# The output projection of an attention layer's last two quarters as seven block products

## The chip, the cores and the metric

The kernel runs on one core of a Trainium2 chip. The metric is device time in microseconds (us) of one execution of the whole program. The kernel before takes 2368.16 us, the median of three runs between 2368.03 and 2368.29.

## The reference

One layer of a streaming encoder on 2048 tokens of width 1024, in float32: an attention in chunks of 64 tokens (each reads its own chunk and the eight before it, 16 heads of 64) with an output projection, then a dense SwiGLU network of inner width 2816. Both are wrapped in two RMS norms.

```python
h = rms_norm(x, g_pre_mix)
o = attention(h, w_qkv, rel_bias)             # softmax(q k / 8 + bias) v, 16 heads merged to 1024
x = x + rms_norm(o @ w_o, g_post_mix)
h = rms_norm(x, g_pre_ffn)
x = x + rms_norm((silu(h @ w_gate) * (h @ w_up)) @ w_down, g_post_ffn)
```

The change is about `o @ w_o`, 1024 by 1024, and what reads its result.

## The kernel before, in words

Everything is kept transposed: a tile has 128 features in its partitions and 512 tokens in its columns. The 2048 tokens are four quarters of 512 (`NQ`) and two groups of 1024 (`NG`). A float32 product is three matmuls of 512 columns (`products`, L195): each operand is split in a high part (ScalarE) and a low part (VectorE), and high by high, high by low and low by high are added in one bank of PSUM. Below, such three matmuls are a triple.

Most large products use a scheme of Strassen and Winograd: operands are cut in two by two blocks, and seven block products with sums of blocks (named B11, B21, T1, T2, B22, T3, T4 for the column side, A11, A12, S1 to S4, A22 for the weight side) stand in for eight. The projections of q, k and v do so, the gate and up products (`gate_up`, L995) and the down product. The output projection does not: `o_quarter` (L632) runs, for one quarter, eight output tiles with eight triples each, 64 triples, and ends every tile with a copy to DRAM (`o_d`) and a square added to the row sum (`osums`) that the later norm needs.

The stages follow each other: q, k, v for both groups; the attention of the quarters in the order 1, 0, 2, 3 (`SEQ_OF`); a dense stage; the FFN of group 0 (gate and up in eleven chunks of 56 triples, then down) and of group 1. A quarter of the attention has eight jobs, one per pair of heads, of four slots each, one per block of 128 queries (loop at L1635). A slot issues the transposes of one block (`transposed`, L571), in every second slot the transposes of the fifth key block, the scores of the block three slots ahead (`scores`, L522) and a share of the dense work at hand (`fill`, L1613). After the fourth slot of a pair comes its output product (`output`, L605), whose result ScalarE copies as high part and VectorE as low part into `ats`. From the second quarter on, both heads of a pair write their scores to one tile of three PSUM banks (`later_banks`, L459). The dense work between a quarter's scores is the output projection of the quarter before; the first quarter has none, and the projection of the last quarter is the dense stage behind the attention. There VectorE and ScalarE also build the first columns B11, B21 and T1 of the FFN (`Blocks.build`, L721), with their parts of x1 loaded as L11 to L22.

What sets the order: TensorE's is the order of the program text. Steps of other engines are queued in `later` with a cost each and issued as the generators of TensorE's work advance (`tick`, L206, one unit per triple); a scheduler places them on their engines, with the steps of the softmax and the output copies put ahead. Loads and most stores go through one queue, SyncE's (SP), in order; stores of weight sums and additions in DRAM go through GpSimd's (POOL). Weight tiles come from `take` (L177) with splits at fixed triples (`part_split`, L151) in the attention, and from a `Stream` (L889) that loads six items ahead and splits three ahead elsewhere. `weight_sums` (L862) forms the S blocks of the down weights by copies and adding transfers within DRAM, one step per eight triples, 40 of them in the projection stage, the rest in the first FFN. `Late` (L1188) adds a quarter's projection to x: from `osums` (`rows`) or from sums formed anew out of `o_d` (`sums`, `rstd`), and `write`.

## Time and profile before

| | |
|---|---|
| median of three runs | 2368.16 us |
| profiled execution: its time / its span | 2367.66 us / 2365.9 us |
| busy over the span: PE, PEld | 2318.8 us (98%), 1898.9 us (80%) |
| DVE, ACT, POOL | 1634.0 us (69%), 1141.5 us (48%), 324.5 us (14%) |
| mean granted TensorE clock | 0.996 |
| DMA | 531.80 MB, mean 225 GB/s |

PE is TensorE's matmuls, PEld its weight loads, DVE is VectorE, ACT ScalarE, POOL GpSimd, SP SyncE. Times within the execution count from its first instruction. Matmuls are pipelined: the duration of a record is longer than the step from one start to the next, and the steps are what a sum is made from. The bracket at the end of a row gives the idle time of the engine before it and what ended it. Names such as `tt`, `pd` or `hb` are tiles; `po`, the output product's bank, appears as `tt`.

The last quarter's attention lies from 882 to 1041.5 us, the dense stage from there to 1086.2, the first chunk of gate and up to 1124.3.

### The profile page before, as it was taken

The page shows a single profiled execution, that of the slowest core. Times are in us where ns is not written, and L with a number is a line of the kernel's source. Part 1 is how long each engine was busy: PE and PEld are TensorE (multiplying, and loading weights), DVE is VectorE, ACT ScalarE, POOL GpSimd, SP SyncE. Part 2 cuts the span into 40 slices and gives each one's busy share as a digit, 9 for nine tenths or more (in the row PEclk, how much of TensorE's full clock was granted, in tenths as well). Part 3 has the DMA queues.
Part 4 walks back from the last instruction along what each step waited for, and adds up shares of the span by engine and source line. Part 5 has one row for each costly group of instructions (what it writes and reads, how often), then busy time and mean ns, then how long its engine had stood idle before and what let it go on. Part 6 is the DMA issues. An engine that isn't in the chain of part 4 may idle for free.

```text
span 2365.9 us, 32865 instructions
## 1 busy us (share of the span) xinstructions
PE 2318.8 (98%) x11456; PEld 1898.9 (80%) x11456; DVE 1634.0 (69%) x2620; ACT 1141.5 (48%) x1979; POOL 324.5 (14%) x426
## 2 busy tenths in 40 slices
PE   9999999989999999999999999999999999999998
PEld 7788888877777778778888888888888888888886
DVE  8787856667566665769786877667657676555577
ACT  7544643367666566665323333455433333334444
POOL 1000011044333433511100000000000000000001
PEclk9999999999999999999999999999999999999999
DMA  8777799998897888766876454567666656547654
GB/s 302 250 254 270 241 280 263 281 261 232 218 254 218 242 261 253 240 216 221 281 245 215 168 200 152 178 209 249 222 226 194 216 171 225 155 164 233 196 189 145
DMA packets 231509, 531.80 MB, mean 225 GB/s; under 512 B 26512, under 2 KB 42912, under 8 KB 226864
## 3 DMA queue, kind: packets, MB, share of 16 engines
q1 hardware_dynamic: 219440, 482.52, 64.1%
q0 software_dynamic: 11904, 47.19, 7.0%
q8 instruction: 90, 1.47, 0.3%
q14 instruction: 75, 0.61, 0.1%
HBM read 382.23 MB, written 170.44 MB: 234 GB/s over the span
## 4 chain that ended last, share of the span: by engine, by line
PE 68%; DVE 2%; DMA 2%; ACT 1%; issue 1%; POOL 0%; SPq 0%; DVEq 0%
PE pd L197 6%; PE pd L199 6%; PE pd L198 6%; PE pb L197 5%; PE pb L199 5%; PE pb L198 5%; PE tt L618 3%; PE pc L197 3%; PE pc L198 3%; PE pa L198 3%; PE pc L199 3%; PE pa L199 3%; PE pa L197 3%; PE tt L582 2%; PE mm L197 2%; PE mm L199 2%
## 5 line engine op out<-in xcount | busy, mean ns | idle before, releaser
L567 POOL TENSOR_SCALAR sc<-sc,rows 128x640 f32<-128x640 f32 (+4 forms) x256 | 199.1, 792 | 303.9 <-DVE rows L563 240.2
L553 ACT ACTIVATE sc<-sc,rows 128x640 f32<-128x640 f32 (+4 forms) x256 | 193.2, 757 | 91.6 <-DVE rows L548 90.5
L197 PE MATMUL pb<-hb,w_wg_T 128*128 128x512 f32 x528 | 205.9, 390 | 1.2 <-DVE terms L1045 1.1
L199 PE MATMUL pb<-hb,w_wg_T 128*128 128x512 f32 x528 | 205.4, 389 | 0.0
L198 PE MATMUL pb<-hb,w_wg_T 128*128 128x512 f32 x528 | 205.4, 389 | 0.0
L548 DVE CUSTOM_DVE_ANT_0 sc<-st,bias 128x640 f32<-128x640 f32 (+2 forms) x248 | 174.1, 734 | 45.2 <-PE st L539 19.6
L538 PE MATMUL st<-k,q 128*128 128x384 f32 (+3 forms) x432 | 138.4, 337 | 13.3 <-DVE rows L548 11.4
L586 DVE COPY pT<-tt 128x512 f32<-128x512 f32 (+3 forms) x128 | 81.7, 638 | 84.5 <-PE tt L582 82.8
L199 PE MATMUL pd<-a,w_d_T 128*128 128x512 f32 (+1 forms) x368 | 139.8, 380 | 0.1
L197 PE MATMUL pd<-a,w_d_T 128*128 128x512 f32 (+1 forms) x368 | 139.9, 380 | 0.0
L198 PE MATMUL pd<-a,w_d_T 128*128 128x512 f32 (+1 forms) x368 | 139.7, 380 | 0.0
L197 PE MATMUL pa<-hb,w_wg_B 128*128 128x512 f32 x352 | 136.9, 389 | 0.0
L198 PE MATMUL pa<-hb,w_wg_B 128*128 128x512 f32 x352 | 136.9, 389 | 0.0
L199 PE MATMUL pa<-hb,w_wg_B 128*128 128x512 f32 x352 | 136.9, 389 | 0.0
L582 PEld LDWEIGHTS tt<-ident,sc 128*128 128x128 f32 x928 | 105.2, 140 | 37.2 <-POOL sc L567 15.7
L131 ACT ACTIVATE w_wg_T<-raw 128x1024 fp32r<-128x1024 f32 x88 | 93.1, 1058 | 80.0 <-PE pa L199 34.5
L582 PE MATMUL tt<-ident,sc 128*128 128x128 f32 x928 | 125.8, 275 | 5.3 <-DVE rows L563 2.5
L539 PE MATMUL st<-k,q 128*128 128x384 f32 (+3 forms) x432 | 125.6, 311 | 0.0
L289 POOL TENSOR_TENSOR rs<-ms,neg_half 128x4 f32<-128x4 f32 (+1 forms) x7 | 7.5, 1072 | 856.8 <-DVE ms L287 856.8
L357 DVE TENSOR_TENSOR a<-raw_a,a 128x512 fp32r<-128x512 f32 x154 | 105.8, 694 | 26.8 <-ACT a L356 26.7
L1047 ACT ACTIVATE terms<-terms 128x512 f32<-128x512 f32 x65 | 41.1, 632 | 170.5 <-DVE terms L1045 170.4
L618 PE MATMUL tt<-pT,v 128*64 128x512 f32 (+3 forms) x832 | 119.9, 438 | 0.0
(277 smaller groups left out, 6171.5 us busy)
## 6 DMA issues: line engine op xcount, KB each, us to landing
raw<-in_w_gu SPq DMA_DIRECT2D x77, 512.0 KB, 4.2
q<-q SPq DMA_DIRECT2D x62, 512.0 KB, 6.4
k<-k SPq DMA_DIRECT2D x54, 512.0 KB, 8.1
s_g_S<-raw POOLq DMA_DIRECT2D x44, 512.0 KB, 3.0
raw_d<-d_S SPq DMA_DIRECT2D x88, 256.0 KB, 3.7
raw_a<-aT SPq DMA_DIRECT2D x88, 256.0 KB, 3.8
raw<-s_g_S SPq DMA_DIRECT2D x44, 512.0 KB, 4.0
bias<-ext_d SPq DMA_DIRECT2D x124, 144.0 KB, 8.9
```

The source lines that it names most:

```text
L131: act.activation(hi, raw, AF.Copy)
L197: pe.matmul(pt, a_hi, b_hi, start=first, stop=False, skip_group_check=go_on)
L198: pe.matmul(pt, a_hi, b_lo, start=False, stop=False, skip_group_check=go_on)
L199: pe.matmul(pt, a_lo, b_hi, start=False, stop=last, skip_group_check=go_on)
L357: eng.tensor_tensor(lo, src, hi.bitcast(F32), op=ALU.subtract)
L538: pe.matmul(st[:, a:b], q[:, 2 * h, cols], kk[:, h, key], start=True, stop=False)
L539: pe.matmul(st[:, a:b], q[:, 2 * h + 1, cols], kk[:, h, key], start=False, stop=True)
L548: dve.tensor_tensor_reduce(out=sc[:, :n], in0=st[:, c0 : c0 + n], in1=rev, scale=-1.0, scalar=3.0e38, op0=ALU.add, op1=ALU.min, accum_out= ...
L553: act.activation(sc[:, :n], sc[:, :n], AF.Exp, bias=nmax, scale=-1.0, accum_out=rows[:, h : h + 1])
L567: last_pool[0] = pool.tensor_scalar(sc[:, :n], sc[:, :n], rows[:, 2 + h : 3 + h], 1.0, op0=ALU.mult, op1=ALU.mult)
L582: pe.transpose(tt[:, u, :], sc[h][:, b * P : b * P + P], ident)
L618: pe.matmul(po[heads[h], c0:c1], v[:, kb, c : c + 64], self.pT[:, h, r, c0:c1], start=m == 0, stop=m == len(terms) - 1,)
```

## The change

The last two quarters (2 and 3 in order of tokens, the third and fourth to be worked on) are taken as two column blocks of one product, the halves of the features as the other cut, and the scheme of seven block products replaces the two runs of 64 triples. A block product is four output tiles with four triples each.

- Two products, A11 and A12 by the third quarter's own columns, run between the scores of the last quarter (`o_first`); the first is kept in DRAM as p1, the second added to it gives the upper output rows of the third quarter.
- Five, S1, S2, S3, S4 and A22 by T1, T2, T3, B22 and T4, run in the dense stage (`o_rest`); here these column names mean differences of the two quarters' attention outputs. T1 is prepared in the slots of the last quarter, T2, T4, T3 and B22 during the first of the five. Results are formed on VectorE from p1 and the banks.
- The third quarter's output is stored a second time, in float32, to `at_d`, and loaded again for the differences (`Columns`); the fourth is kept in float32 without a low part.
- The S blocks of the output weights are formed by `weight_sums` ahead of the down weights', in two pieces of 128 by 1024.
- The FFN's first columns B11, B21 and T1 are issued later in the dense stage, into other tiles.
- Row sums of the last two quarters no longer come from the projection; `Late` forms them from `o_d` in the first FFN.

```diff
...
+    at_d = dram.tile([P, KT, HALF], F32, name="at")
+    p1_d = dram.tile([P, 4, HALF], F32, name="p1")
+    sum_o = {n: [dram.tile([P, 1024], F32, name=f"o_{n}_{c}") for c in range(2)] for n in ("S1", "S2", "S3", "S4")}
...
-    plan = [w_o[c] for c in range(4)] * NQ
+    halves_of = [w_o[c][:, n : n + 1024] for c in range(4) for n in (0, 1024)]
+    o_at = {n: [halves_of[i], halves_of[i + 2]] for n, i in (("A11", 0), ("A12", 1), ("A21", 4), ("A22", 5))}
+    plan = [halves_of[2 * c : 2 * c + 2] for c in range(4)] * (NQ - 2) + [o_at["A11"], o_at["A12"], sum_o["S1"]]
...
-            sp.dma_start(part, plan[n][:, here])
+            sp.dma_start(part, plan[n][c])
...
+            if n == SEQ_OF[-1]:
+                if p == 0:
+                    ats[n] = hb_tile(2, F32, (KT, HALF))
+                with tc.high_priority(offset=400):
+                    act.activation(ats[n][:, p, :], po, AF.Copy)
+                return lambda: None
             if p == 0:
                 ats[n] = Cols(((0, 1), (2, 3))[SEQ_OF.index(n) % 2])
             with tc.high_priority(offset=400):
                 act.activation(ats[n].hi(p), po, AF.Copy)
+            if n == SEQ_OF[-2]:
+                t = io("at")
+                with tc.high_priority(offset=400):
+                    act.activation(t, po, AF.Copy)
+                sp.dma_start(at_d[:, p, :], t)
...
     def o_quarter(n):
 
         src = ats[n]
-        last = n == SEQ_OF[-1]
         osums[n] = row_tile("osum", f"osum_{n}") if SEQ_OF.index(n) % 2 else const.tile([P, HALF], F32, name=f"osum_{n}", tag="osum", bufs=1)
...
-            if last and d2 == KT // 2 - 1:
-                back.ahead(-2)
...
+    def o_first(src):
+
+        for half in range(2):
+            w = take()
+            for d in range(4):
+                pt = dense_bank(d)
+                if half:
+                    p1 = io("p1")
+                    sp.dma_start(p1, p1_d[:, d, :])
+                for k in range(4):
+                    hi, lo = w.tiles[d // 2]
+                    c = slice(k * 256 + d % 2 * P, k * 256 + d % 2 * P + P)
+                    products(pt, hi[:, c], lo[:, c], src.hi(4 * half + k), src.lo(4 * half + k), k == 0, k == 3)
+                    yield 3 * C512
+                    if (d, k) == (2, 3):
+                        part_split(0)
+                    elif (d, k) == (3, 2):
+                        part_split(1)
+                if half:
+                    dve.tensor_tensor(p1, p1, pt, op=ALU.add)
+                    sp.dma_start(o_d[SEQ_OF[-2]][:, d, :], p1)
+                else:
+                    t = io("y")
+                    act.activation(t, pt, AF.Copy)
+                    sp.dma_start(p1_d[:, d, :], t)
+
+    class Columns:
+
+
+        def __init__(self):
+            self.at2 = hb_tile(3, F32, (KT, HALF))
+            self.at3 = None
+            self.t = {}
+
+        def load(self, half):
+            here = slice(4 * half, 4 * half + 4)
+            sp.dma_start(self.at2[:, here, :], at_d[:, here, :])
+
+        def t1(self, k):
+            dve.tensor_tensor(self.at2[:, k, :], ats[SEQ_OF[-1]][:, k, :], self.at2[:, k, :], op=ALU.subtract)
+
+        def others(self, k, which=range(3)):
+            at2, at3 = self.at2, ats[SEQ_OF[-1]]
+            if 0 in which:
+                dve.tensor_tensor(at2[:, k, :], at3[:, 4 + k, :], at2[:, k, :], op=ALU.subtract)
+            if 1 in which:
+                dve.tensor_tensor(at2[:, 4 + k, :], at2[:, 4 + k, :], at2[:, k, :], op=ALU.subtract)
+            if 2 in which:
+                dve.tensor_tensor(at3[:, k, :], at3[:, k, :], at3[:, 4 + k, :], op=ALU.subtract)
+
+        def put(self, name, k):
+            slot, src, at, sign = {
+                "T1": (0, self.at2, k, 1), "T2": (1, self.at2, k, 1), "T4": (6, self.at2, 4 + k, 1),
+                "T3": (4, ats[SEQ_OF[-1]], k, 1), "B22": (5, ats[SEQ_OF[-1]], 4 + k, -1),
+            }[name]
+            if name not in self.t:
+                self.t[name] = hb_tile(slot)
+            hi, lo = (self.t[name][:, n, k, :] for n in range(2))
+            if sign > 0:
+                split(hi, lo, src[:, at, :])
+                return
+            act.activation(hi, src[:, at, :], AF.Copy, scale=-1.0)
+            dve.scalar_tensor_tensor(lo, src[:, at, :], -1.0, hi.bitcast(F32), op0=ALU.mult, op1=ALU.subtract)
+
+    def o_items():
+
+        def load(src):
+            t = phase["fp"].tile([P, 1024], F32, tag="w4", name="raw4", bufs=phase["w4"])
+            sp.dma_start(t, src)
+            return t
+
+        def make(name, t):
+            w = w_tile(f"o_{name}")
+            split_part(*w, t)
+            return w
+
+        return [
+            (lambda src=src: load(src), lambda t, n=n, c=c: make(f"{n}_{c}", t), 6, 3)
+            for n, both in (("S2", sum_o["S2"]), ("S3", sum_o["S3"]), ("S4", sum_o["S4"]), ("A22", o_at["A22"]))
+            for c, src in enumerate(both)
+        ]
+
+    def o_rest(cols):
+
+        first, second = SEQ_OF[-2:]
+        roots = [bank("prs").rearrange("p (a b) -> p a b", a=4) for _ in range(2)]
+        banks_y = [ps.tile([P, HALF], F32, tag="mm", name="pd") for _ in range(2)] + [bank("pd") for _ in range(2)]
+        banks_x, terms = [], {}
+
+        def product(pts, name, begin, slab, after):
+            b = cols.t[name]
+            for d in range(4):
+                if d % 2 == 0:
+                    hi, lo = slab[d // 2] if slab else back.take()
+                elif slab and d == 3:
+                    back.ahead(-2)
+                for k in range(4):
+                    c = slice(k * 256 + d % 2 * P, k * 256 + d % 2 * P + P)
+                    products(
+                        pts[d], hi[:, c], lo[:, c], b[:, 0, k, :], b[:, 1, k, :],
+                        begin and k == 0, k == 3, not begin,
+                    )
+                    yield 3 * C512
+                after(d)
+
+        def one(d):
+            return terms["one"][:, d, :]
+
+        def two(d):
+            return terms["one"][:, 4 + d, :]
+
+        def three(d):
+            return terms["two"][:, d, :]
+
...
+        def begin():
+            terms["one"] = hb_tile(3, F32, (KT, HALF))
+            sp.dma_start(terms["one"][:, 0:4, :], p1_d)
+
+        def second_terms():
+            terms["two"] = hb_tile(2, F32, (KT, HALF))
+
+        def after_t2(d):
+            dve.tensor_tensor(two(d), one(d), banks_x[d], op=ALU.subtract)
+
+        def after_t3(d):
+            dve.tensor_tensor(three(d), banks_x[d], one(d), op=ALU.subtract)
+            dve.tensor_tensor(three(d), three(d), banks_y[d], op=ALU.add)
+            store(second, 4 + d, three(d))
+
+        def after_b22(d):
+            dve.tensor_tensor(two(d), two(d), banks_y[d], op=ALU.subtract)
+            store(second, d, two(d))
+
+        def after_t4(d):
+            dve.tensor_tensor(one(d), banks_x[d], one(d), op=ALU.subtract)
+            store(first, 4 + d, one(d))
+
+        def put(name):
+            return [(0.8, lambda k=k: cols.put(name, k)) for k in range(4)]
+
+        later.extend(
+            put("T2") + put("T4") + [(0.0, begin)] + blocks[0].spreads(lambda name: roots.pop(0))
+            + put("T3") + put("B22") + [(0.0, second_terms)]
+        )
+        slab = take().tiles
+        back.ahead(-4)
+        yield from product(banks_y, "T1", True, slab, lambda d: None)
+        while "two" not in terms:
+            later.popleft()[1]()
+        banks_x.extend(bank("pd") for _ in range(4))
+        yield from product(banks_x, "T2", True, None, after_t2)
+        yield from product(banks_x, "T3", False, None, after_t3)
+        yield from product(banks_y, "B22", False, None, after_b22)
+        yield from product(banks_x, "T4", False, None, after_t4)
+
...
-        def spreads(self):
+        def spreads(self, bank=norm_bank):
...
-                spread(self.r[t], row)
+                spread(self.r[t], row, bank)
 
...
-        def long(t):
-            return t.rearrange("(a b) c -> a (b c)", b=2)
-
-        def copy(to, a):
+        def long(t, wide):
+            return t.rearrange("(a b) c -> a (b c)", b=2) if wide else t
+
+        def copy(to, a, wide):
             with tc.issue_after(last_sp[0].ins):
-                last_sp[0] = nc.sync.dma_start(long(to), long(a), max_dma_last_dim=8192)
-
-        def add(to, a):
+                last_sp[0] = nc.sync.dma_start(long(to, wide), long(a, wide), max_dma_last_dim=8192)
+
+        def add(to, a, wide):
             with tc.issue_after(last_pool[0].ins):
-                pool.dma_start(long(to), long(a), accum_op=ALU.add, max_dma_last_dim=8192)
-
-        steps = [[] for _ in range(4 * len(units) + 16)]
-        for u, (src, dst) in enumerate(units):
+                pool.dma_start(long(to, wide), long(a, wide), accum_op=ALU.add, max_dma_last_dim=8192)
+
+        both = [({n: o_at[n][c] for n in o_at}, {n: sum_o[n][c] for n in sum_o}) for c in range(2)]
+        steps = [[] for _ in range(4 * len(units) + 24)]
+        for u, (src, dst) in enumerate(both + units):
             at = 8 * (u // 2) + u % 2
+            wide = u >= 2
             for n, (to, a) in enumerate((("S1", "A21"), ("S3", "A11"), ("S2", "A11"), ("S4", "A12"))):
-                steps[at + 2 * n].append((copy, dst[to], src[a]))
+                steps[at + 2 * n].append((copy, dst[to], src[a], wide))
             for n, to, a in ((2, "S1", src["A22"]), (4, "S2", dst["S1"]), (5, "S3", src["A21"]), (7, "S4", dst["S2"])):
-                steps[at + 2 * n].append((add, dst[to], a))
+                steps[at + 2 * n].append((add, dst[to], a, wide))
         for step in steps:
-            yield [f(to, a) for f, to, a in step]
+            yield [f(*args) for f, *args in step]
 
 
...
-                    later.extend(lates[n].rows(5.0) + lates[n].write(12.0))
-                later.extend(pause(24.0) + blocks[1].sums(10.0, True))
+                    later.extend(lates[n].sums(5.0) + lates[n].rstd(1.5) + lates[n].write(10.0))
+                later.extend(pause(16.0) + blocks[1].sums(10.0, True))
...
-        Blocks([x1_d[2 * g + t] for t in range(2)], PRE_FFN, ((0, 3, 5, 4, 6, 1, 2), (0, 1, 2, 3, 4, 5, 6))[g])
+        Blocks([x1_d[2 * g + t] for t in range(2)], PRE_FFN, ((5, 3, 0, 1, 4, 2, 6), (5, 2, 6, 3, 1, 0, 4))[g])
...
-    front, items = Stream(items), []
+    front, items = Stream(items), o_items()
...
+    cols = None
...
+                if n == NQ - 2:
+                    work, left[0] = o_first(ats[SEQ_OF[n]]), left[0] / 2
+                    cols = Columns()
+                    cols.load(0)
...
+        if cols is not None:
+            s = t % per
+            if s == 6:
+                cols.load(1)
+            if s in (5, 9, 13, 17):
+                cols.t1(s // 4 - 1)
+            elif s in (18, 19, 22, 23):
+                cols.put("T1", (18, 19, 22, 23).index(s))
+            elif s in (21, 25, 29):
+                cols.others(s // 4 - 5, (0,))
+            elif s in (26, 27, 30):
+                cols.others((26, 27, 30).index(s), (1, 2))
+            tick(1.0)
...
+    cols.others(3)
...
     first = lambda part, w: blocks[0].build(part, w, lambda t, k, x_: blocks[0].norm(x_, t, k))
-    for part in ("L11", "L21", "L12", "L22"):
-        first(part, 0.0)[0][1]()
-        if part == "L11":
-            fetch()
-    later.extend(blocks[0].spreads() + timed(
-        (3.0, first("B11", 2.5)), (15.0, first("B21", 2.5)), (28.0, first("T1", 4.0))
-    ))
-    for c in o_quarter(NQ - 1):
+    work, done = o_rest(cols), 0.0
+    for c in work:
+        if done == 0.0:
+            later.extend(timed(
+                (2.0, first("L11", 0.0)), (2.0, first("L12", 0.0)), (18.0, first("L21", 0.0)), (18.0, first("L22", 0.0)),
+                (33.0, first("B11", 2.5)), (49.0, first("B21", 2.5)), (58.0, first("T1", 2.0)),
+            ))
         tick(c / (3 * C512))
+        done += 1.0
     drain()
...
```

3 lines of the change are left out of this document (2 added, 1 removed).

## The prediction

> **What bounds the kernel now.** I read first the busy time by stage: the first quarter of the attention, which has no projection between its scores; the last quarter; the dense stage behind it; the first chunk of gate and up. The columns are length, then busy time and (instructions) of PE, PEld, DVE, ACT, POOL, then granted clock, DMA share and GB/s.
>
> ```profile
> 498.00:601.00 103.00, 98.34 (x720) 79.99 (x718) 69.83 (x178) 74.56 (x166) 44.17 (x57) 1.00 0.86 226
> 882.00:1041.50 159.50, 155.22 (x1023) 122.83 (x1021) 101.49 (x217) 99.27 (x205) 62.45 (x69) 1.00 0.73 222
> 1041.50:1086.20 44.70, 44.70 (x201) 36.80 (x201) 40.21 (x54) 26.43 (x41) 1.73 (x3) 1.00 0.78 284
> 1086.20:1124.30 38.10, 38.10 (x176) 31.70 (x175) 37.16 (x54) 23.29 (x37) 4.99 (x7) 1.00 0.61 191
> ```
>
> TensorE is busy in all four, and VectorE is nearly as busy in the last two: 40.21 of 44.7 us and 37.16 of 38.1. So a gain must shorten TensorE's list, and in those two stages VectorE stands right behind it. Next, whether TensorE's list really sets the pace among the scores. Below are the first and the last of eight output products (values times probabilities, one per pair of heads) of the first quarter and of the last, and then all that TensorE waited for in the last quarter.
>
> ```profile
> 498.43 4.53 PE L618 MATMUL tt<-pT,hb 128*64 128x512 f32 x32
> ...
> 601.14 4.53 PE L618 MATMUL tt<-pT,v 128*64 128x512 f32 x32
> ```
>
> ```profile
> 897.95 2.37 PE L618 MATMUL tt<-pT,v 128*64 128x512 f32 x16
> ...
> 1036.63 4.89 PE L618 MATMUL tt<-pT,v 128*64 128x512 f32 x32
> ```
>
> ```profile
> PE st L538 <- DVE rows L548: 2.6, 4, 1.1
> PE st L538 <- DMA k<-k: 1.3, 1, 1.3
> PE mm L197 <- ACT sq L264: 0.4, 1, 0.4
> ```
>
> Seven pairs take 102.7 us without projection (14.67 each) and 138.7 us with it (19.81). The difference, 5.14 us, is nearly the eight triples of projection that a pair carries (5.44 us, priced next). TensorE waited only 4.3 us in 159.5. Work taken from between the scores is therefore time saved, until a wait grows.
>
> **Price of a product.** The start of the first product of the first gate and up chunk, and of its sixth, T3; five products of 24 matmuls lie between:
>
> ```profile
> 1086.21 0.39 PE L197 MATMUL pa<-hb,w_wg_B 128*128 128x512 f32 x1
> ...
> 1113.41 0.39 PE L197 MATMUL pb<-hb,w_wg_T 128*128 128x512 f32 x1
> ```
>
> 27.2 us for 120 matmuls: 0.227 us each, 0.68 us a triple (three matmuls of one product of high and low parts). A block product is 16 triples, 10.9 us. The two quarters cost eight block products now and seven after: one leaves for good. But they also move: among the last quarter's scores stand four now and two after (-21.8 us), in the dense stage four now and five after (+10.9 us).
>
> **Part 1, the last quarter.** Its average load doesn't bind: VectorE loses four splits of weights (8 to 4), seven additions to the row sum and eight low halves and gains 21 additions and splits of the columns and of p1, so it stays near 101 us of some 143. DMA loses 2 MB of weights and 1 MB of stores and gains 4 MB (p1 out and in, the third quarter's columns), so 0.73 of 159.5 us becomes about 0.82 of 143; the first quarter ran at 0.86. What binds is the turn of the score bank. Rows of TensorE and VectorE around two changes of slot:
>
> ```profile
> 884.17 0.34 PE L539 MATMUL st<-k,q 128*128 128x384 f32 x1
> 885.41 0.82 DVE L548 CUSTOM_DVE_ANT_0 sc<-st,bias 128x640 f32<-128x640 f32 x1
> 886.29 0.44 PE L538 MATMUL st<-k,q 128*128 128x384 f32 x1 [0.42 <-DVE rows L548]
> ```
>
> ```profile
> 947.83 0.34 PE L539 MATMUL st<-k,q 128*128 128x384 f32 x1
> 948.00 0.39 PE L197 MATMUL mm<-hb,w 128*128 128x512 f32 x1
> 949.39 1.04 PE L582 MATMUL tt<-ident,sc 128*128 128x128 f32 x8
> 950.18 0.42 PE L538 MATMUL st<-k,q 128*128 128x384 f32 x1
> ```
>
> Both heads share one score tile. VectorE reads it in two passes (the second is shown) that begin when the last score matmul is through, so the next scores start at the earliest 2.12 us after the start of the last one (884.17 to 886.29). Now two triples (1.39 us) and eight transposes (0.79 us) fill that gap to 2.35 us. With one triple it is 1.67 us, and TensorE waits 0.45 us; in slots that also issue the fifth transposes it comes to 2.1 us, no wait and no slack; the slot with the output product is long anyway. One bare slot per pair, eight pairs: 3.6 us. Then VectorE's lateness, which slack hid until now. What its two passes waited for besides TensorE in the last quarter:
>
> ```profile
> DVE sc L548 <- POOL sc L567: 5.7, 5, 1.4
> DVE sc L548 <- issue: 1.9, 3, 0.9
> ```
>
> Of these 7.6 us TensorE felt 2.6 (above). Between no more lateness and all of it I take 4.0. So the waits become 3.6 + 4.0 in place of 2.6: +5.0 us, bounds +1.0 (3.6 - 2.6) and +8.6 (3.6 + 7.6 - 2.6).
>
> **Part 2, the dense stage and the chunk behind it.** VectorE's price per instruction is the step from one start to the next in an unbroken stretch of the stage:
>
> ```profile
> 1061.82 0.74 DVE L707 SCALAR_TENSOR_TENSOR hb<-hb,gt,row 128x512 f32<-128x512 f32 x1
> 1062.48 1.22 DVE L132 TENSOR_TENSOR w<-raw,w 128x1024 fp32r<-128x1024 f32 x1
> 1063.62 0.68 DVE L357 TENSOR_TENSOR hb<-hb,hb 128x512 fp32r<-128x512 f32 x1
> 1064.22 1.22 DVE L132 TENSOR_TENSOR w<-raw,w 128x1024 fp32r<-128x1024 f32 x1
> ```
>
> 0.66 us for 512 columns with a gain, 1.14 for a tile of weights, 0.60 for 512 columns. After the change the dense stage has 54.4 us of TensorE (five times 10.9) and asks of VectorE: three last columns and twelve low halves (9.0), four negated ones (2.6), eight weight tiles (9.1), twenty sums with the products' banks (12.0), the FFN's columns B11, B21 and T1 (twelve norms 7.9, sixteen others 9.6), three gate weights with their sums (6.8): 57.0 us. Before: the same FFN columns (17.5), six weight tiles (6.8), row sum and a low half (5.4), two gate weights with sums (4.5): 34.2 us. From there until the FFN's T3 columns are ready it is 28.0 us after (columns 19.4, reads of banks 3.0, five weight tiles 5.7) and 30.3 before (two weight tiles more). Up to that point VectorE has 85.0 us against 64.5, so 20.5 more, while TensorE gets there only 10.9 us later: 9.6 us short. What can take it up is seen in the end of the T3 columns now and in the only wait of TensorE in that chunk:
>
> ```profile
> 1111.04 1.89 DVE L357 TENSOR_TENSOR hb<-t,hb 128x512 fp32r<-128x512 f32 x3
> ```
>
> ```profile
> PE pb L197 <- DVE terms L1045: 1.1, 1, 1.1
> ```
>
> The columns end at 1112.9; product T3 starts at 1113.41 and reads the last of them 2.0 us later, so 2.5 us are spare. VectorE now idles 4.5 us in the dense stage. After the change it still waits at the start for the copy of the last output (0.6), and later for the FFN's first columns, whose tile is free only when product T1 ends at 10.9 us. They take
>
> ```profile
> hb<-x SPq DMA_DIRECT2D x4, 1024.0 KB, 10.6
> ```
>
> 10.6 us to land, at 21.5, while the work that can be done before then (columns, S2, S3 and one S4 tile, three sums) fills it to about 20: some 2.5 us idle by my estimate, 2.0 recovered. 9.6 - 2.5 - 2.0 = 5.1 us of new TensorE waits, of which 1.1 is paid already: +4.0 us. The bound below is -1.1 (all of it fits and the old wait goes too), above +9.0 (the second rival). ScalarE doesn't bind there: 26.4 us now, and it loses sixteen copies and squares of 0.6.
>
> A long wait costs more than itself. Two waits, and the windows with the clock behind each:
>
> ```profile
> 475.10 0.60 PE L538 MATMUL st<-hb 128*128 128x384 f32 x1 [2.25 <-DVE rows L548]
> ```
>
> ```profile
> 836.63 0.50 PE L197 MATMUL mm<-hb,w 128*128 128x512 f32 x1 [4.32 <-ACT sq L264]
> ```
>
> ```profile
> 475.00:480.00 5.00, 4.90 (x17) 4.36 (x18) 3.10 (x11) 3.47 (x8) 1.62 (x3) 0.66 0.98 220
> 836.00:839.00 3.00, 2.37 (x6) 1.55 (x6) 2.09 (x4) 1.58 (x4) 1.93 (x2) 0.67 0.85 225
> ```
>
> After 2.25 us of waiting the granted clock was 0.66 for 5 us, 1.7 us lost; after 4.32 us it was 0.67 in the next 3 us, 1.0 us lost at least. In the forecast the 5.1 us are spread over the waits of three products' columns, each under 2 us, and I add nothing. The Trainium skill, "TensorE: Matmul & The Clock Gate", Part 1 (the HAM clock gate), says that the array falls to half its clock after an idle window of about 3.4 us; by it alone a 2.25 us wait would cost nothing more, and here it did, so the trace decides. By the page's threshold the sum stays as it is too, as no wait of the forecast is that long.
>
> **Part 3, what else moves.** Third quarter: ScalarE copies each output product a second time and SP stores it, eight times. The copy is 0.60 us:
>
> ```profile
> 1041.56 0.60 ACT L625 ACTIVATE hb<-tt 128x512 fp32r<-128x512 f32 x1 [4.12 <-PE tt L618]
> ```
>
> Its bank is wanted again a slot later, about 3.6 us, which covers it; without that cover 8 x 0.60 = 4.8 us. The stores share three buffers and SP's queue with the loads of heads behind them; the 4.32 us wait above is one of that quarter, and the reshuffled order may lose it (-4.3) or get another (+4.8). I take +0.7. Projection of q, k, v: the sums of two pieces of the output weights put 16 transfers of 512 KB on SP's and POOL's queues, into a stretch that reads
>
> ```profile
> 320.00:340.00 20.00, 20.00 (x90) 16.57 (x89) 9.46 (x12) 9.15 (x12) 4.67 (x6) 1.00 1.02 310
> ```
>
> The DMA engines are full there and TensorE loses nothing: weights are loaded six tiles ahead, 5.4 us each, and that covers it; without the cover 4 MB more at 310 GB/s would be 13 us. The FFN: eight steps of down weights' sums come later there, and the last two quarters' row sums are formed anew, two times about 19 VectorE instructions of 0.60 us, 23 us over ten chunks of 38.1 us. VectorE's spare is smallest right behind the dense stage, and the step starts after it. Both together +0.6, bounds 0 and +3.
>
> **The sum.** -21.8 + 5.0 + 10.9 + 4.0 + 0.7 + 0.6 = -0.6 us. The profiled execution took 2367.66 us, 1.8 around its span, and the three timed runs have the median 2368.16, 0.5 more. I forecast 2367.1 for such an execution, **2367.6** as a median: the block product saved is eaten by waits on VectorE. About 0.2% (4.7 us) is what a measurement of this kernel can tell from no change; the forecast's own range, 2363.4 to 2372.9, is that.
>
> ```profile
> span 2365.9 us, 32865 instructions
> ```
>
> **Rivals.**
> Faster: VectorE's order fits, and both its terms come to their lower bounds. -21.8 + 1.0 + 10.9 - 1.1 + 0 = -11.0, so 2357.2 at the lowest; half way from there to the forecast it is 2362.4. For it: VectorE is free a third of the last quarter, and every wait listed there is short. Against: 97% busy in the first chunk, and one wait a pair that follows from the score tile alone.
> Slower: VectorE's backlog decides, in the first chunk. If the FFN's columns are not prepared earlier than TensorE's order issues them, then to the last block product of the dense stage (10.9 us) fall 19.2 us: B21 and T1 (12.5), four sums (2.4), two gate weights (4.5). VectorE enters the chunk 8.3 us late, T3's columns come at 54.4 + 8.3 + 28.0 = 90.7 us of the stage in place of 54.4 + 27.2 = 81.6; with 1.0 us of its usual idle that is +10.1, less 1.1 paid, +9.0. Such waits exceed 2.25 us, so the clock falls, twice 1.7: -21.8 + 5.0 + 10.9 + 9.0 + 3.4 + 1.3 = +7.8, 2376.0. It decides once TensorE waits about 8 us in the chunk. For it: the 9.6 us above. Against, VectorE's norms of FFN columns between 1041.5 and 1085:
>
> ```profile
> L707 DVE SCALAR_TENSOR_TENSOR hb<-hb,gt,row 128x512 f32<-128x512 f32 x16 | 11.7, 745 | 0.6 <-ACT row L347 0.6
> ```
>
> Twelve belong to B11, B21 and T1; the other four are T2's, issued only behind the stage and yet done inside it. VectorE's order is not bound to TensorE's.
> No relief: the last quarter keeps its pace, and the five blocks come on top. 10.9 + 4.0 + 1.3 = +16.2, 2384.4. Against: 14.67 us a pair without projection.
>
> **How the numbers follow.** Forecast 0.37, faster 0.35, backlog 0.23, no relief 0.05. Their sides give faster 0.35, same 0.37, slower 0.28. Cases of both signs hold most of the chance. The range reaches from 2358 (all but the last of the faster case) to 2377 (just past the backlog's 2376.0); no relief and what lies beyond on both sides, some 0.17, stay out.
>
> **What would show it.** In the profile after: pairs of the last quarter at about 17.7 us (19.81 - 2.73 + 0.6) between output products; waits of the scores on VectorE's passes of about 7.6 us in that quarter, mostly near 0.45; a dense stage of about 55 us without long waits; in the first chunk TensorE waiting some 5 us for low halves of columns, T2 to T3; the clock at 1.00 there. Wrong it would be if pairs stay near 20 us, if the score waits stay under 3 us, if the first chunk keeps 38 to 39 us, or if a wait of the third quarter or of the projection's weights comes that is not in the sum.

## The result, and the profile after

| | us |
|---|---|
| before, five runs of this comparison | 2368.16 (2365.70 to 2369.08) |
| after, five runs | 2411.78 (2407.26 to 2413.69) |
| ratio | 1.0183, 95% interval 1.0168 to 1.0198 |

The kernel became 43.6 us slower. The forecast was 2367.6, in a range from 2358 to 2377. The profiled execution after is the fastest of its five, 2407.26 us, so what follows explains 39.6 us over the profiled one before (2367.66).

The windows of the changed kernel, with the columns used before: the third quarter of the attention, the last, the dense stage, chunks 0 and 1 of gate and up.

```profile
735.00:891.00 156.00, 141.98 (x919) 113.58 (x917) 95.15 (x205) 96.64 (x199) 60.22 (x64) 0.95 0.83 246
891.00:1053.70 162.70, 141.71 (x928) 108.12 (x924) 101.26 (x224) 95.46 (x199) 61.99 (x70) 0.95 0.77 222
1053.70:1109.20 55.50, 55.50 (x249) 45.93 (x249) 52.02 (x72) 25.61 (x38) 1.72 (x3) 1.00 0.83 306
1109.20:1154.80 45.60, 40.99 (x169) 33.17 (x168) 45.37 (x66) 24.79 (x38) 3.94 (x6) 0.93 0.39 117
1154.80:1195.00 40.20, 39.03 (x172) 31.79 (x171) 30.27 (x42) 15.59 (x23) 8.05 (x11) 1.00 0.97 302
```

TensorE has 141.71 us of work in a last quarter of 162.7, where before it had 155.22 in 159.5: the work went, the time stayed. In both quarters its clock fell to 0.95. Only the dense stage is what the forecast said: 55.5 us, TensorE never idle, clock 1.00.

For every run the time is split at four marks on TensorE: the last output product of a quarter, and the first product of a chunk. "Last" is the last quarter, "dense" runs from its last output product to chunk 0, "chunks" from the start of chunk 0 to that of chunk 10. What lies ahead of these marks is 1.2 us shorter after than before, and what lies behind them agrees.

| | third | last | dense | chunks (first six intervals) |
|---|---|---|---|---|
| before | 164.4 | 158.9 | 49.6 | 386.3 (39.5 39.5 39.5 38.1 38.1 38.1) |
| after | 174.9 | 161.8 | 60.3 | 403.0 (45.6 40.1 46.7 38.6 38.5 40.2) |
| difference | +10.5 | +2.9 | +10.7 | +16.7 |
| forecast | +0.7 | -16.8 | +10.9 | +4.6 |

What TensorE waited for in the changed kernel: first the third quarter, then the last, then chunks 0 to 5 (us in total, times, longest).

```profile
PE tt L586 <- DVE hb L643: 9.1, 2, 8.8
PE tt L586 <- POOL sc L571: 4.3, 1, 4.3
...
PE st L542 <- DMA k<-k: 8.7, 5, 4.8
PE st L542 <- DVE rows L552: 4.7, 7, 1.1
PE mm L201 <- DVE p L687: 3.5, 1, 3.5
...
PE pb L201 <- DVE terms L1217: 7.6, 3, 4.6
PE pb L202 <- DVE hb L361: 2.9, 1, 2.9
PE pb L201 <- ACT hb L360: 1.7, 1, 1.7
```

The dense stage grew as forecast. So there are four places to explain: the third quarter, the last, chunk 0 and the chunks behind it. The wait that the forecast was built on, scores on VectorE's passes (`st <- DVE rows`), came with 4.7 us for 7.6 foreseen; the largest ones it did not hold.

### The profile page after: what moved, and what is told of

Its sections match the earlier page's. It is cut to its first block, busy times and chain, and to the rows that moved or that the text cites. A ratio compares the mean times of both kernels' runs of the same rounds, so it can differ in the third digit from the quotient of the medians.

```text
span 2405.5 us, 32939 instructions
## 1 busy us (share of the span) xinstructions
PE 2321.7 (97%) x11388; PEld 1897.5 (79%) x11388; DVE 1673.5 (70%) x2692; ACT 1146.9 (48%) x1995; POOL 328.3 (14%) x432
## 4 chain that ended last, share of the span: by engine, by line
PE 59%; DMA 6%; DVE 6%; issue 2%; ACT 1%; SPq 1%; POOL 0%; DVEq 0%; POOLq 0%; ACTq 0%
PE pd L201 6%; PE pd L203 6%; PE pd L202 6%; PE pb L201 4%; PE pb L202 4%; PE pb L203 4%; PE pa L202 3%; PE pa L201 3%; PE tt L622 3%; PE pa L203 3%; PE pc L202 3%; PE pc L201 3%; PE pc L203 3%; PE tt L586 2%; PE st L542 2%
## 5 line engine op out<-in xcount | busy, mean ns | idle before, releaser
L571 POOL TENSOR_SCALAR sc<-sc,rows 128x640 f32<-128x640 f32 (+4 forms) x256 | 196.9, 784 | 318.1 <-DVE rows L567 244.6
L201 PEld LDWEIGHTS pb<-hb,w_wg_T 128*128 128x128 f32 x528 | 100.3, 190 | 34.3 <-issue 9.3
```

The costliest lines, as they stand in the source:

```text
L201: pe.matmul(pt, a_hi, b_hi, start=first, stop=False, skip_group_check=go_on)
L571: last_pool[0] = pool.tensor_scalar(sc[:, :n], sc[:, :n], rows[:, 2 + h : 3 + h], 1.0, op0=ALU.mult, op1=ALU.mult)
```

## The experiments

A stage is compared within one trace; the total of a single run is good to about 4 us, as the kernel before lay between 2364.1 and 2371.6 over all sessions.

**The second copy of the third quarter, and the queue of the last: e1, e2, e3.** These are the row of the 8.8 us wait and what leads to it, from the timeline of the changed kernel (start, duration, instruction, idle time before and what ended it):

```profile
785.00 2.91 POOL L1404 TENSOR_TENSOR y<-res,y 128x512 f32<-128x512 f32 x2
786.72 0.60 ACT L639 ACTIVATE at<-tt 128x512 f32<-128x512 f32 x1 [4.10 <-POOL y L1404]
787.35 0.69 DVE L643 TENSOR_TENSOR hb<-tt,hb 128x512 fp32r<-128x512 f32 x1 [1.78 <-ACT at L639]
...
788.19 1.94 PE L586 MATMUL tt<-ident,sc 128*128 128x128 f32 x8 [8.82 <-DVE hb L643]
```

The new copy takes a buffer of the kind `io`, which rows of x still hold until GpSimd has added to them (L1404). ScalarE stands at the copy, VectorE's low half of the same output product stands behind it, and TensorE needs the product's bank for its transposes. In the last quarter it is SyncE's queue, whose instructions the same view lists as `SPq`:

```profile
949.13 0.32 SPq L72 DMA_DIRECT2D x<-y  x1
949.72 0.32 SPq L72 DMA_DIRECT2D y<-o  x1
950.32 0.33 SPq L72 DMA_DIRECT2D res<-in_x  x1
960.67 0.32 SPq L72 DMA_DIRECT2D x<-y  x1
...
964.42 0.32 SPq L72 DMA_DIRECT2D x<-y  x1
964.79 0.61 SPq L72 DMA_DIRECT2D q<-q  x1
965.45 1.26 SPq L72 DMA_DIRECT2D k<-k  x2
```

Between 950.65 and 960.67 the queue issues nothing: at its head is a store of x1 (`x<-y`), which waits for GpSimd's addition, 959.36 to 960.65. That addition stands in GpSimd's order behind the masks of the scores (L571), which wait for VectorE: GpSimd idled 5.80, 2.44 and 1.66 us between 946.31 and 959.36. Behind the store in SyncE's queue stand the keys of the next pair of heads, issued at 965.45; TensorE then waits 4.84 us for them at 974.9. The Trainium skill, "Perfetto Trace Analysis", section "Per-instruction lifecycle", puts the semaphore wait of a transfer into the issuing sequencer, ahead of the profiled row; the ten empty microseconds ahead of this store agree.

e1 takes the copy away and loads both halves of the split instead; e2 moves the stores that follow GpSimd's additions to GpSimd's own queue; e3 does both.

```diff
# e1
-                t = io("at")
-                with tc.high_priority(offset=400):
-                    act.activation(t, po, AF.Copy)
-                sp.dma_start(at_d[:, p, :], t)
+                sp.dma_start(at_d[:, p, :], ats[n].hi(p).bitcast(F32))
...
+                    sp.dma_start(lo_d[:, p, :], ats[n].lo(p).bitcast(F32))
...
+            last_pool[0] = pool.dma_start(self.at2[:, here, :], lo_d[:, here, :], accum_op=ALU.add)
# e2
-                sp.dma_start(self.dst[:, dt, :], y)
+                (pool if eng is pool else sp).dma_start(self.dst[:, dt, :], y)
```

> The third quarter's output is stored from the high and low parts themselves (two stores, added on loading), so ScalarE's second copy and its io buffer are gone; the arithmetic is the same. Theory Q (queues held in order by a short buffer): the 8.8 us and 4.3 us TensorE waits of the third quarter go, the last output product of that quarter comes about 10 us earlier (877 instead of 887 us), the last quarter stays near 162 us, total 2398 to 2402. Theory L (the load itself, VectorE and DMA, is too much for pairs shorter than 20 us): the waits stay in other places, total 2407 to 2414.

> The stores of x1 that follow GpSimd's addition between the scores go through GpSimd's own queue instead of SyncE's; nothing else changes. Theory Q: SyncE's queue is no longer held behind GpSimd, so the loads of k come on time; k waits of the last quarter fall from 8.7 to under 2 us, the clock there returns to about 1.00 from 0.95, and the last quarter falls from 162 to about 145 us; total about 2394. Theory L: the last quarter stays at 158 us or more, total over 2405.

> Both edits together. Theory Q: the gains add up, third quarter 10 us and last quarter 17 us shorter, total about 2384; what is left over the kernel before is the dense stage (+10.8) and the FFN chunks (+16.7). Theory L: total over 2400.

e1 took 2430.6 us: third 178.0, last 177.9. A miss: with eight more stores on SyncE's queue and accumulating loads on GpSimd's, the last quarter has longer waits than those removed, 12.8 us for keys and one of 7.6 for ScalarE (`osum`). e2 took 2396.5: third 169.5, last 147.4. In its last quarter no wait for keys is left; in its third one of 7.8 us behind the new copy remains. e3 took 2399.1: 167.1 and 158.7. In e3's last quarter the waits for keys are gone as well, but one of 8.2 us for `osum` stands (1.8 in the changed kernel); what in e1's way of loading leads to it was not followed. So SyncE's queue is shown by e2 (14.3 us in the last quarter by one moved line), the buffer not yet.

**Does half the filling shorten the last quarter? e4, e5.** On the kernel before, half of the products of the projection between the last quarter's scores are left out; e5 also does without the addition to x that runs there.

```diff
# e4
+                    if n == SEQ_OF[-2] and k % 2:
...
+                        continue
# e5, beside that
+                    if n == NQ - 2:
+                        sp.dma_start(late.dst, late.res)
+                    else:
+                        later.extend(pause(5.0) + late.rows(4.0) + late.write(3.0, pool, 1))
```

> The kernel before, but of the third quarter's projection only every second feature block is multiplied, so that half the products stand between the last quarter's scores; the other half is left out. It prices the relief alone. The forecast: last quarter from 158.9 to about 142 us (relief 21.8, score bank 3.6, VectorE's lateness 1.4), total 2351. Theory Q: SyncE's queue is held behind the x1 stores here too, and shorter pairs expose it: last quarter 150 to 156 us, k waits of 4 us or more, total 2359 to 2365. Theory L: 158 us, total 2367.

> The kernel before with half of the third quarter's products (as in the run with half the filling), and besides without the residual addition that runs between the last quarter's scores: its eight loads, GpSimd additions and stores are left out, and x is copied to x1 in one transfer within DRAM. Theory Q (the queues of SyncE, ScalarE and VectorE, held in order behind that addition's steps, cost what the shorter pairs gain): pairs of about 17.1 us throughout, last quarter 137 to 141 us, total 2348 to 2352. Theory L (VectorE and DMA can't feed pairs of 17 us): last quarter 150 us or more, total over 2360.

e4: last quarter 157.9 us, where before it was 158.9. Half of TensorE's filling gone, and 1 us gained. Its pairs take 17 to 18 us until the second of the additions, then 28.4, 23.9 and 21.9. TensorE waits 4.9 us for keys there and 6.7 for ScalarE's squares (`sq`), so SyncE's queue is part of what takes the gain, not shown to be all of it. e5: 137.7 us, with 132.3 us of TensorE's work where before it was 154.6. The relief is real, and without the additions and their stores it is larger than the forecast's 16.8 us; what leaving out the additions gives by itself, with the whole projection in place, no run shows.

**Both causes taken away cleanly: e6, e7.** In e6 GpSimd adds high and low part within SBUF to form the float32 columns, eight instructions, with no copy, store or load; e7 is e6 with the stores of e2.

```diff
...
-            sp.dma_start(self.at2[:, here, :], at_d[:, here, :])
+            pool.tensor_tensor(self.at2[:, k, :], src.hi(k).bitcast(F32), src.lo(k).bitcast(F32), op=ALU.add)
```

> The changed kernel, but the third quarter's output in float32 is formed in the last quarter by eight GpSimd additions of its high and low parts, which lie in SBUF; the second copy on ScalarE, its buffer, its store and the load are gone. Theory Q: the third quarter returns to 164 to 166 us between its bounding output products (174.9 in the changed kernel, 164.4 before), total about 2400. Theory L: 170 us or more.

> The same with the stores of x1 between the scores on GpSimd's queue. Theory Q: third quarter 164 to 166 us, last quarter 145 to 148 us, total about 2386. Theory L: third quarter 170 or last quarter 155 us and more.

e6: third 163.4, where before it was 164.4: the second copy, with its buffer, store and load, cost all of the 10.5 us. The last quarter fell too, to 154.2, though the stores of x1 stay where they were; waits for keys fell from 8.7 to 3.0 us. Total 2391.7. e7: third 158.4, last 148.4, total 2379.1; the stores on GpSimd's queue shorten the third quarter as well. So the two causes overlap: the copy with its stores and loads costs 7.6 us in the last quarter as long as the stores stand in SyncE's queue, and the stores cost 5 us in the third. Beside the dense stage's forecast 10.7 us, what is left of the loss stands in chunks 0 to 5: 45.1, 40.5, 46.0, 38.7, 38.5, 41.8 us.

**Chunk 0 and the chunks behind it: e8, e9, e10, e12.** e8 is the kernel before with nothing but the new row sums of the last two quarters in the FFN. e9 is e7 with the sums of gate and up weights on GpSimd; e10 adds eight subtractions behind T2 there. e12 is e7 with VectorE's eight low halves of S2 to A22 replaced by copies on ScalarE.

```diff
# e8
-                    later.extend(lates[n].rows(5.0) + lates[n].write(12.0))
+                    later.extend(lates[n].sums(5.0) + lates[n].rstd(1.5) + lates[n].write(10.0))
# e9
-            dve.tensor_tensor(r[to], r[a], r[b], op=op)
+            (pool if key[0] == "g" else dve).tensor_tensor(r[to], r[a], r[b], op=op)
# e10, beside that
-                joined(b, b, k, c, ALU.subtract)
+                joined(b, b, k, c, ALU.subtract, pool)
# e12
-            split_part(*w, t)
+            act.activation(w[0], t, AF.Copy)
+            act.activation(w[1], t, AF.Copy)
```

> The kernel before with one edit: the FFN forms the row sums of the last two quarters anew, with the changed kernel's costs, in place of those from the projection. Theory F1 (the chunks are long because VectorE brings a backlog out of the dense stage): the eleven chunks grow by at most 3 us, total 2368 to 2372. Theory F2 (the new sums, their loads and the writes behind them are the larger part): chunks 1 to 9 grow by 7 to 11 us, total 2376 to 2381.

> As the run with the parts and the x1 stores on GpSimd's queue (2379 us), and the four sums of gate and up weights of each chunk of the first FFN are formed on GpSimd, which is idle there, in place of VectorE: 3 of them in the dense stage (3.4 us of VectorE), 4.6 us of VectorE per chunk after it. Theory F1 (VectorE's backlog from the dense stage is the cause of all 17 us, first by late columns, then by loads that wait in SyncE's queue behind late stores): chunk 0 falls from 45 to 41 us, the eleven chunks together from 404 to about 392, total 2367. Theory F3 (the loads of the new row sums and writes crowd SyncE's queue in any case): chunk 0 falls, chunks 1 to 5 keep their 10 us, total 2374.

> The same, and the eight subtractions behind T2's columns in chunk 0 on GpSimd as well (4.8 us of VectorE). Theory F1: chunk 0 at 38.5 to 40 us, the eleven chunks 386 to 389 us (386.3 in the kernel before), total 2361 to 2364. Theory F3: chunks 1 to 5 keep 10 us, total about 2372.

> As the run with the parts and the x1 stores on GpSimd's queue (2379 us), but the low halves of the eight weight tiles of S2, S3, S4 and A22 are copies made by ScalarE; the subtraction is left out, 9.1 us of VectorE in the dense stage, and nothing else is moved. Theory F1 (VectorE's backlog is the cause of all of the FFN's 17 us): chunk 0 at 38.5 to 40 us, the eleven chunks 385 to 390 us, total 2362 to 2366. Theory F3 (the loads of new sums and writes crowd SyncE's queue in any case): chunk 0 falls to about 39, chunks 1 to 5 keep 10 us, total about 2372.

e8: 2364.7, chunks 385.0; the row sums cost nothing in the kernel before. e9: 2395.3, chunks 419.7, e10: 2399.0 and 424.8, both slower than e7's 403.9; a reason is told in the last section. e12: 2380.0, chunk 0 at 43.5. In it VectorE is busy 45.37 of 55.4 us of the dense stage, so it has idle time there, and chunk 0 gained 1.6 us for some 9 us of work taken off (eight times 1.14); the chunks together took 406.5 us, 2.6 more than in e7. So the amount of work in the dense stage isn't what delays chunk 0. VectorE is busy without a break in chunk 0, in e12 too (43.42 of 43.5 us): what counts is the work left for it when the stage ends. Part of that is seen in VectorE's norms, grouped over two windows of the changed kernel, dense stage and chunk 0 (count, busy us, mean ns, idle before):

```profile
L877 DVE SCALAR_TENSOR_TENSOR hb<-hb,gt,row 128x512 f32<-128x512 f32 x12 | 8.8, 744 | 0.0
...
L877 DVE SCALAR_TENSOR_TENSOR hb<-hb,gt,row 128x512 f32<-128x512 f32 x4 | 2.9, 742 | 0.0
```

Before, sixteen such norms lay in the dense stage; now four of them, T2's, lie in chunk 0. They stand in VectorE's order behind the last sums with the banks, and those end only with TensorE's last product; three rows of VectorE from the timeline:

```profile
1111.10 0.68 DVE L805 TENSOR_TENSOR hb<-pd,hb 128x512 f32<-128x512 f32 x1
...
1115.18 1.40 DVE L877 SCALAR_TENSOR_TENSOR hb<-hb,gt,row 128x512 f32<-128x512 f32 x2
...
1140.95 2.49 DVE L361 TENSOR_TENSOR hb<-t,hb 128x512 fp32r<-128x512 f32 x4
```

Chunk 0 holds 45.37 us of VectorE's work in 45.6, where before it held 38.51 in 39.45, and the last low halves of T3's columns run from 1140.95, behind TensorE's start of that product (waits of 1.7 and 2.9 us). Whether the four norms come late by VectorE's order alone, or because T2's tile is not free sooner, no run tells apart.

**What crowds chunks 1, 2 and 5: e13, e14, e15.** On e7, the steps for the rows of the last two quarters (e13), those for the sums of down weights (e14), or both (e15) begin later.

```diff
# e13, e15
-                later.extend(pause(12.0))
+                later.extend(pause(190.0))
# e14, e15
-        if 40.0 < done and done % 8.0 < 1.0:
+        if 170.0 < done and done % 8.0 < 1.0:
```

> The kernel with both attention edits (second copy formed by GpSimd adds, x1 stores on GpSimd's queue; 2379.1 us, its first eleven chunk starts 403.9 us apart: 45.1, 40.5, 46.0, 38.7, 38.5, 41.8 ...), with one edit: the steps for the last two quarters' rows (sums, root, addition to x) start about 190 triples into the first FFN, not 12. Crowding by these steps: chunk 0 keeps about 45, chunks 1, 2 and 5 fall to 38 to 39, all ten intervals to about 391 to 394, total about 2368 to 2371. Chunk 0's lateness carried on, or the down-weight steps: chunks 1 to 5 stay within 2 us in sum of what they were (40.5, 46.0, ...), total 2377 to 2381; if the crowding is only moved, chunks 4 to 7 lengthen by what chunks 1 to 5 lose.

> The same base (2379.1 us), with one edit: the steps that form the sums of down weights (loads, stores and adding transfers within DRAM) start 170 triples into the first FFN, not 40. If these transfers, 8 steps more of them since the output weights' sums went first, hold up the loads in chunks 1 to 3: chunk 2 falls from 46.0 to below 41, total about 2371 to 2374. If the rows' steps or chunk 0's lateness are the cause: chunks 1 to 5 within 2 us in sum of before, total 2377 to 2381.

> Both edits: rows' steps from 190 triples, down-weight steps from 170. If one of them alone is the cause, this is as fast as that one (within 2 us), unless both then meet from chunk 3 on. If it is chunk 0's lateness carried on in VectorE's order, chunk 1 and chunk 2 stay at 40 and 46 with both taken out: total 2377 or more. If either is enough to crowd the chunks, only this run comes to 2368 to 2371.

First six intervals: e13 45.1, 38.1, 38.1, 38.1, 38.5, 38.1; e14 45.1, 38.5, 40.1, 47.5, 41.2, 47.7; e15 45.1, 38.1, 38.1, 38.1, 38.5, 42.2. Chunk 0's lateness is not carried on: in e13 and e15 chunk 1 is clean behind the same chunk 0. In e14 the loss moved along with the start of the down-weight sums, to chunks 3, 4 and 5. The rows' steps without these transfers cost next to nothing (chunks 4 to 9 of e13), the start of the down-weight sums alone nothing (chunks 1 to 3 of e13): the large losses stand where both run together. The transfers keep the DMA engines busy (0.97 in chunk 1 of the changed kernel), and rows and weight tiles come late to VectorE, which waits for them in order; three such rows of the changed kernel's chunk 2, and among them TensorE's longest wait there, for a bank that VectorE had not read yet:

```profile
1214.92 1.23 DVE L1109 TENSOR_TENSOR raw<-raw,raw 128x1024 f32<-128x1024 f32 x1 [4.06 <-DMA raw<-in_w_gu]
...
1224.66 0.75 DVE L1401 SCALAR_TENSOR_TENSOR y<-y,gt,total 128x512 f32<-128x512 f32 x1 [1.95 <-DMA y<-o]
...
1233.66 0.77 PE L201 MATMUL pb<-hb,w_wg_T 128*128 128x512 f32 x1 [4.58 <-DVE terms L1217]
...
1237.27 0.75 DVE L1401 SCALAR_TENSOR_TENSOR y<-y,gt,total 128x512 f32<-128x512 f32 x1 [2.03 <-DMA y<-o]
```

That both start in the same chunks is not enough, though. They do so in e8, without loss. One difference is the number of transfers: the output weights' sums went first, so more of the down weights' are left for the FFN. In its first 190 us, in the changed kernel and then in e8 (destination and source, queue, count, size, median us from issue to landing):

```profile
d_S<-d_S POOLq DMA_DIRECT2D x9, 256.0 KB, 6.6
d_S<-in_w_d SPq DMA_DIRECT2D x9, 256.0 KB, 5.2
d_S<-in_w_d POOLq DMA_DIRECT2D x8, 256.0 KB, 7.9
...
d_S<-d_S POOLq DMA_DIRECT2D x5, 256.0 KB, 6.6
d_S<-in_w_d POOLq DMA_DIRECT2D x4, 256.0 KB, 6.9
d_S<-in_w_d SPq DMA_DIRECT2D x3, 256.0 KB, 3.4
```

They are 26 for 12. Nor is that the whole: in e15 about as many transfers and the rows' steps start together in chunk 3, and the chunks lose some 4 us by it. What sets the size of the loss stays open.

In total e13 gained nothing, 2381.1 us; e14 took 2387.2 and e15 2383.9. e13 won 14.5 us up to chunk 10 and lost 16.6 behind it. Its rows' steps had not ended when the chunks did; the next group's columns came late:

```profile
1520.70 0.80 PE L317 MATMUL sum<-hi,ones 128*128 128x512 f32 x1 [12.28 <-ACT hi L359]
```

**All these delays but chunk 0's taken away, and the same for the kernel before: e16, e17, e11.** e16 starts the rows' steps at 85 triples, e17 at 130 with the next group's sums closer behind. e11 is the kernel before with the store of e2 and the sums of e8, without the change.

> The base with both attention edits (2379.1 us), and the rows' steps from 85 triples into the first FFN, 1.5 chunks, so that they end before the eleven chunks do (in the run from 190 triples they did not, and TensorE waited 12.3 us for the next group's first columns right behind the chunks). If what crowds chunks 1, 2 and 5 is the meeting of the rows' steps with the start of the down-weight sums (whose busy time on GpSimd stands in the first four chunks), part of it stays here, as the start lies in chunk 1 and 2 still: chunk 2 or 3 at 40 to 44, no 12.3 us wait, total 2366 to 2372. If it is the rows' steps alone: the same losses a chunk and a half later, total 2377 to 2381.

> The same with the rows' steps from 130 triples, 2.3 chunks, and the next group's sums set closer behind them so that these too end in time. Meeting theory: chunks 1 to 10 at 38 to 40, the first eleven starts 390 to 394 us apart, no wait of 12 us behind them, total 2363 to 2368, at most level with the kernel before (2368 to 2372 in these sessions), and above the kernel before with x1 stores on GpSimd's queue (2359.8), since the dense stage's five block products and chunk 0 (17 us) outweigh the last quarter's gain (10.5 us against that kernel's 158.9). Rows' steps alone: total 2377 or more.

> The kernel before with two pieces taken from the runs: the x1 stores between the scores on GpSimd's queue, and the row sums of the last two quarters formed in the FFN. The projection stays as it was. Theory Q: the third quarter loses its 4.3 us wait and the slower clock behind it (164.4 to about 158.5 us between its bounding output products), the eleven chunks fall by 1 to 2 us as in the run with the new sums alone; total 2359 to 2362. Theory L: the stores only move the wait, total 2364 to 2368.

| | third | last | dense | chunks | median | ratio to before, 95% |
|---|---|---|---|---|---|---|
| e16 | 157.7 | 147.0 | 60.3 | 391.7 | 2366.2 (10 runs) | 0.9995, 0.9986 to 1.0005 |
| e17 | 157.7 | 147.1 | 60.3 | 394.2 | 2368.4 (10 runs) | 1.0005, 0.9996 to 1.0014 |
| e11 | 157.8 | 158.9 | 49.6 | 385.5 | 2359.8 (5 runs) | 0.9965, 0.9951 to 0.9980 |

Chunk 0 is still at 45.1 in both. e17's chunks 3 and 4 are at 41.3 and 40.0, though chunk 4 holds none of the transfers, so the rows' steps are not always free. With the other delays gone the change makes no difference to the kernel before, and part of that is the moved store, which the kernel before can have too. Against e11 the change in e16 gives 11.9 us in the last quarter and costs 10.7 in the dense stage and 6.2 in the chunks: 5 us lost. e11 is faster than both kernels.

## Why the prediction was wrong

**The sum was nearly that of another kernel.** 2367.6 us is about what e16 and e17 show, but in part by luck: in e16 the third quarter is 6.7 us shorter than before, by the moved store that no term held, and the last is 4.9 us longer than the forecast's 142.1. The prediction priced engines by their work and TensorE's waits on VectorE, and left out what in-order queues do with late work. By its steps:

- *Block products, -21.8 and +10.9.* Right. The dense stage came at 55.5 us for "about 55", and in e5 TensorE's work among the scores is 22.3 us less than before.
- *Waits on the score tile, 3.6 + 4.0 - 2.6.* The mechanism was right, the size somewhat large: 4.7 us in 7 waits where 7.6 were foreseen. But the step counted VectorE alone. In e16, where the copy is gone and the stores of x1 are on GpSimd's queue, the last quarter has three more, 6.1 us, which the sum did not hold (the waits of TensorE in that quarter of e16):

```profile
PE st L541 <- DVE rows L551: 4.9, 9, 1.1
PE mm L200 <- DVE p L681: 3.5, 1, 3.5
PE tt L602 <- ACT osum L350: 1.8, 1, 1.8
PE tt L602 <- DVE ms L290: 0.8, 2, 0.4
```

- *"Its average load doesn't bind."* This is the step that failed in the last quarter. It put load against time for VectorE and the DMA engines, and asked of no queue what stands behind the waiting instruction. The stores of x1 waited in SyncE's queue for GpSimd's additions, the keys behind them came late (e2), and TensorE's waits came to 21.0 us (161.8 less 140.8 of work) where 9.3 follow from the forecast. TensorE's work itself was 8.0 us longer than 154.6 - 21.8, at a clock of 0.95. 11.7 and 8.0 are the 19.7 us by which the step missed. Before, SyncE's queue waited for these additions as well, 19.2 us in the last quarter for 25.7 now, and TensorE waited only 1.3 us for keys. That the shorter pairs turned the one into the other is argued, not tested. The rival "no relief", at 0.05, came true in its effect, by a mechanism that the prediction did not name.
- *Third quarter, +0.7, bounds -4.3 and +4.8.* Missed: +10.5. "Its bank is wanted again a slot later, which covers it" looked at ScalarE's 0.60 us, and not at what the copy needs first. That the stores share three buffers was written down; that rows of x hold these buffers until GpSimd is done was not followed.
- *Chunk 0, +4.0, bounds -1.1 and +9.0.* Place and size were about right: T3's columns, two waits of 1.7 and 2.9 us, 6.1 us with the clock at 0.93. The working behind it was not: it counted work in VectorE's dense stage, and e12 shows that taking 9 us of it away gives 1.6. What weighs is what is left for VectorE when the stage ends. "VectorE's order is not bound to TensorE's", said against the backlog rival, fell with the four norms of T2. The 1.1 us wait quoted as chunk 0's is the next chunk's: `pb <- DVE terms` is at 1159.56. So nothing was "paid already" in chunk 0, and the prediction's own working gives +5.1.
- *FFN, +0.6, bounds 0 and +3.* Missed: +10.6 in chunks 1 to 9. The prediction set the row sums against VectorE's spare time and named the eight later down-weight steps without a price of their own. That 26 transfers for 12 run together with the rows' steps, and that VectorE's loads come late then, was in no term; e13 shows it by keeping the two apart. How much of the 10.6 us comes from the number of transfers stays open.
- *Clock.* "I add nothing" was wrong in both quarters and in chunk 0 (0.93), for the waits in the quarters were longer than foreseen. Before, 2.25 us of waiting brought the clock to 0.66 for 5 us; here, with waits of up to 8.8 and 4.8 us, the mean of two whole quarters is 0.95.

Of the signs that the prediction named for its being wrong, two showed: pairs of 20.2 us on average, and a wait of the third quarter that is not in the sum. Of those for its being right, the clock of 1.00 in the first chunk failed.

## What to carry to other kernels

When work moves, ask of each instruction it adds or brings forward what it must wait for (a buffer, another engine's result) and list what stands behind it in the same engine or queue: here a copy of 0.60 us per pair of heads, with its buffer and store, cost 10.5 us, and the place of a store in a queue some 14. A stretch that TensorE's work set can, once that work is halved, be set by an engine whose busy share looked small; to test it, leave the work out before building the scheme that replaces it (e4 took one run to show that halving alone gains 1 us). And a side task that costs nothing alone need not be free beside another: keeping the two apart won 14.5 us up to chunk 10 (e13), while in e8 they met at no cost, so such a meeting has to be measured.

## What the runs showed of the hardware that was not expected

VectorE was held up by GpSimd. In e9, 40 additions of 1024 columns in the chunks went from VectorE to GpSimd, 1.22 us each on the one, and on the other:

```profile
L1103 POOL TENSOR_TENSOR raw<-raw,raw 128x1024 f32<-128x1024 f32 x40 | 110.9, 2772 | 250.2 <-DVE w_wg_B L136 89.5 <-DMA raw<-in_w_gu 80.3 <-DVE w_wg_T L136 54.4
```

VectorE's busy time in the chunks did not fall, it rose from 325.2 us to 334.4. Two of its groups there, the first with both operands in SBUF, the second with one in PSUM:

```profile
L1222 DVE TENSOR_TENSOR T<-terms,T 128x512 f32<-128x512 f32 x18 | 27.7, 1538 | 0.0
L1211 DVE TENSOR_TENSOR terms<-pb,terms 128x512 f32<-128x512 f32 x36 | 24.1, 681 | 2.4 <-PE pb L202 2.4
```

In e7 the means were 690 and 689 ns. The first group more than doubled, the second stayed. The mean hides two kinds, as the shortest, median and longest of the first group in ns show:

```profile
L1222 DVE TENSOR_TENSOR T<-terms,T x18: 680/685/2890, 1127.4 to 1499.7; 128x512 f32<-128x512 f32 x18
```

Seven of the eighteen took 2.88 to 2.89 us; each of them began 0.43 us after the start of a GpSimd addition and ended 0.55 us behind its end. The others took 0.68 to 0.69. The Trainium skill, "SBUF — State Buffer", section "Who interferes with whom", says that a VectorE instruction with two SBUF inputs contends with a GpSimd instruction that reads SBUF, and calls the ports that the two share an exclusive lock; both groups agree with that. Here, then, work moved from VectorE to GpSimd was not off VectorE's path.
